# An ifftshift copied from memory to memory: 32 DMAs on two queues, or on one

## The chip, the cores and the metric

The kernel runs on one core of one Trainium2 chip. The metric is the time of one execution on the device, in microseconds (us). Two medians are compared, each over several runs.

## The reference

The input is an 8192 x 8192 array of 4-byte floats, 268.4 MB. The output has the same shape and holds the input with both halves of both axes exchanged:

```python
"x": np.random.randn(8192, 8192).astype(np.float32)

def reference(x):
    return np.fft.ifftshift(x)
```

For even sizes this means `out[r, c] = x[(r + 4096) % 8192, (c + 4096) % 8192]`. Nothing is calculated; every byte is read once and written once. One row is 32 KB and one half of a row 16 KB.

## The kernel before

No data enters the core's own memory. Every DMA reads from the device memory and writes to it. The 8192 output rows are cut into 32 blocks of 256 rows, and one DMA moves one block. Its two access patterns, each of the form [step, count] in elements, walk over 256 rows, then over the two halves of a row, then over the 4096 elements of a half. On the output side the halves go left, right. On the input side the walk starts at the right half and steps back by 4096 elements, so it goes right, left. The outermost count, 256, is shared out over the 16 DMA engines: 16 neighbouring rows each, which is 512 KB in 32 pieces of 16 KB.

The helper `whole_rows(queue, block, right_first)` issues one such DMA at L39; `right_first` is always `False` here, so its other branch is not used. The loop over `n` goes through the blocks in groups of four. The sync queue (SP) gets blocks n and n+1, the scalar queue (ACT) blocks n+2 and n+3:

```python
for n in range(0, blocks, 4):
    for a, b in ((0, 2), (1, 3)):
        whole_rows(nc.sync, n + a, False)
        whole_rows(nc.scalar, n + b, False)
```

Each queue thus issues 16 DMAs, and while SP's queue is at block n, ACT's is at block n+2, which is 2 x 8.39 MB further on in both arrays. Both queues feed the same 16 DMA engines. The DMAs don't depend on each other. The framework hands out eight completion semaphores in turn, four to each queue, and before a semaphore is used again the issuing queue waits for the DMA that used it last. So the fifth DMA of a queue waits for its first. At the end SP waits for all of them (L73).

Of the kernel before, what the change touches and what calls it, by code (L numbers as in the profile page):

```python
# [1 line left out]

# [4 lines left out]


ENGINES = 16


@with_exitstack
def kernel(
    ctx: ExitStack,
    tc: tile.TileContext,
    x: bass.AP,
    out: bass.AP,
):


    nc = tc.nc
    R, C = x.shape
    hr = R // 2
    hc = C // 2
    rows = ENGINES * 16
    blocks = R // rows

    def whole_rows(queue, block, right_first):
        row = block * rows
        src = (row + hr) % R  # L30
        to = [[C, rows], [hc, 2], [1, hc]]
        back = [[C, rows], [-hc, 2], [1, hc]]
        if right_first:
            dst, dims, of = hc, back, 0
            dims_of = to
        else:
            dst, dims, of = 0, to, hc
            dims_of = back
        queue.dma_start(  # L39
            out=bass.AP(out.tensor, out.offset + row * C + dst, dims),  # L40
            in_=bass.AP(x.tensor, x.offset + src * C + of, dims_of),
        )

    for n in range(0, blocks, 4):
        for a, b in ((0, 2), (1, 3)):
            whole_rows(nc.sync, n + a, False)
            whole_rows(nc.scalar, n + b, False)


# [1 line left out]
_INS = ['x']  # L51
_OUTS = [((8192, 8192), 'float32')]


# [23 lines left out]
```

## Time and profile before

| what | value |
|---|---|
| median of 3 runs | 865.58 us (865.28 to 866.03) |
| profiled execution, its own time | 868.85 us |
| its span, first to last instruction | 867.1 us |
| busy time of the compute engines | 0.2 us (POOL, four constants that nothing uses) |
| DMA packets | 16896, of which 512 are under 512 B |
| mean rate of the copy | 310 GB/s read, and as much written |

The profile counts every byte of the copy once in its GB/s; the page's line on memory traffic adds reading and writing. A packet is one piece of 16 KB as one of the 16 DMA engines handles it; the 512 small ones report the completions, 16 for each DMA. "q1" is SP's queue and "q10" is ACT's. In the views by windows, the last two columns are the mean busy share of the 16 DMA engines and the rate in GB/s in that stretch; a share slightly over 1.00 comes from packets that reach over the edge of a stretch.

### The profile page before, as it was taken

The numbers are of one execution on the slowest core, as the hardware profiler recorded it, in microseconds if no ns is written. First come the engines' busy times: TensorE is split into PE (matmuls) and PEld (weight loads), VectorE is DVE, ScalarE is ACT, GpSimd is POOL, SyncE is SP. The second block draws the span as 40 slices with busy tenths as digits, with TensorE's granted clock in tenths as the row PEclk, the third lists the DMA queues.
The fourth block names the chain that finished last, engine by engine and source line by source line (L and its number), as shares of the span: only waits on it lengthen the run. The fifth ranks groups of instructions, "written<-read, shape, count | busy, mean of one in ns | idle before, by whom it ended". The sixth has DMA issues, their size and how long they took to land. (4 is left out here: it accounts for less than half of the span.)

```text
span 867.1 us, 77 instructions
## 1 busy us (share of the span) xinstructions
POOL 0.2 (0%) x4
## 2 busy tenths in 40 slices
POOL 0000000000000000000000000000000000000000
DMA  9999999999999999999999999999999999999998
GB/s 280 313 314 305 313 318 312 309 314 309 311 310 315 311 308 305 320 311 313 310 312 316 311 308 313 306 313 310 311 311 314 311 311 317 311 308 309 305 311 273
DMA packets 16896, 268.44 MB, mean 310 GB/s; under 512 B 512, under 2 KB 512, under 8 KB 512
## 3 DMA queue, kind: packets, MB, share of 16 engines
q10 hardware_dynamic: 8448, 134.22, 49.8%
q1 hardware_dynamic: 8448, 134.22, 49.6%
HBM read 268.44 MB, written 268.44 MB: 619 GB/s over the span
## 5 line engine op out<-in xcount | busy, mean ns | idle before, releaser
L62 POOL MEMSET const-bfloat16-1.0<- 128x1 bf16 x1 | 0.1, 102 | 0.0
L62 POOL MEMSET const-uint8-127<- 128x1 uint8 x1 | 0.1, 102 | 0.0
L62 POOL MEMSET const-float32-0.0<- 128x1 f32 x1 | 0.1, 99 | 0.2 <-issue 0.2
L62 POOL MEMSET const-float32-1.0<- 128x1 f32 x1 | 0.1, 99 | 0.0
## 6 DMA issues: line engine op xcount, KB each, us to landing
out_dram<-in_x_dram SPq DMA_DIRECT2D x16, 8192.0 KB, 215.4
out_dram<-in_x_dram ACTq DMA_DIRECT2D x16, 8192.0 KB, 215.4
```

The lines of the kernel that those rows point to most:

```text
L62: nc = _bacc.Bacc("TRN2", target_bir_lowering=False, num_devices=1)
```

## The change

The helper and the grouping go. One loop over the 32 blocks in ascending order issues every DMA on the sync queue; ACT issues none. The access patterns of a block are those of before: the same rows, the same two halves in the same order, the same 16 rows to each engine. All eight completion semaphores now belong to SP's DMAs, so its ninth DMA waits for its first.

```diff
     rows = ENGINES * 16
-    blocks = R // rows
 
-    def whole_rows(queue, block, right_first):
-        row = block * rows
+    for row in range(0, R, rows):
         src = (row + hr) % R
...
-        queue.dma_start(
-            out=bass.AP(out.tensor, out.offset + row * C + dst, dims),
-            in_=bass.AP(x.tensor, x.offset + src * C + of, dims_of),
+        nc.sync.dma_start(
+            out=bass.AP(out.tensor, out.offset + row * C, [[C, rows], [hc, 2], [1, hc]]),
+            in_=bass.AP(x.tensor, x.offset + src * C + hc, [[C, rows], [-hc, 2], [1, hc]]),
         )
-
-    for n in range(0, blocks, 4):
-        for a, b in ((0, 2), (1, 3)):
-            whole_rows(nc.sync, n + a, False)
-            whole_rows(nc.scalar, n + b, False)
```

More of the change, by code (lines that the diff above doesn't have):

```diff
@@ L25 @@
     rows = ENGINES * 16
-    blocks = R // rows
-    def whole_rows(queue, block, right_first):
-        row = block * rows
+    for row in range(0, R, rows):
         src = (row + hr) % R
[L31 to L39, printed above, removed]
-            out=bass.AP(out.tensor, out.offset + row * C + dst, dims),
-            in_=bass.AP(x.tensor, x.offset + src * C + of, dims_of),
-        )
-    for n in range(0, blocks, 4):
-        for a, b in ((0, 2), (1, 3)):
-            whole_rows(nc.sync, n + a, False)
-            whole_rows(nc.scalar, n + b, False)
+        nc.sync.dma_start(
+            out=bass.AP(out.tensor, out.offset + row * C, [[C, rows], [hc, 2], [1, hc]]),
+            in_=bass.AP(x.tensor, x.offset + src * C + hc, [[C, rows], [-hc, 2], [1, hc]]),
+        )
 _INS = ['x']
```

## The prediction

> **What bounds the kernel now.** I began with the page's slices and queues, since nothing is computed:
>
> ```profile
> DMA  9999999999999999999999999999999999999998
> GB/s 280 313 314 305 313 318 312 309 314 309 311 310 315 311 308 305 320 311 313 310 312 316 311 308 313 306 313 310 311 311 314 311 311 317 311 308 309 305 311 273
> DMA packets 16896, 268.44 MB, mean 310 GB/s; under 512 B 512, under 2 KB 512, under 8 KB 512
> q10 hardware_dynamic: 8448, 134.22, 49.8%
> q1 hardware_dynamic: 8448, 134.22, 49.6%
> ```
>
> All 16 DMA engines are busy in every slice, and the two queues share them evenly. The end is set by how long one 16 KB packet occupies an engine: 99.4% of 16 x 867.1 us over 16,384 such packets is 0.84 us. So an idle queue is not what could be repaired here. What can change is the duration of a packet, up or down. The views of the chain and of the waits hold only the four unused constants and SP waiting for DMAs, so I went on to the rate in short stretches. First the two ends of the span, where one queue is alone:
>
> ```profile
> core 0: us, POOL busy (x), PEclk, DMA share, GB/s
> 0.00:2.20 2.20, 0.20 (x4) 1.00 0.20 37
> 2.20:5.40 3.20, 0.00 (x0) 1.00 0.89 307
> 5.40:14.20 8.80, 0.00 (x0) 1.00 1.02 333
> 14.20:27.20 13.00, 0.00 (x0) 1.00 1.00 291
> 860.70:862.70 2.00, 0.00 (x0) 1.00 1.04 295
> 862.70:864.70 2.00, 0.00 (x0) 1.00 0.94 295
> 864.70:867.10 2.40, 0.00 (x0) 1.00 0.11 34
> ```
>
> Up to 5.4 us nearly all packets are SP's, and after 862.7 us all large ones are ACT's. The two microseconds before 862.7 with both queues and the two after it with one have the same 295 GB/s. So one queue can keep the engines moving. Neither end shows that a second queue by itself adds rate.
>
> Then I asked where in a block the rate changes. Two rows give the places of the queues:
>
> ```profile
> start us, us, engine line op out<-in xcount [idle before <-releaser]
> 55.22 46.51 SPq L39 DMA_DIRECT2D out_dram<-in_x_dram  x1
> 60.39 46.02 ACTq L39 DMA_DIRECT2D out_dram<-in_x_dram  x1
> ```
>
> These are the fifth DMAs of the two queues, each held until the queue's first DMA had landed. ACT is 5.2 us behind SP, and one DMA of each queue takes about 54 us. So after each completion there are some 5 us in which SP's packets are at the beginning of a 512 KB piece per engine and ACT's still at the end of one. Half a block later there are again 5 us in which SP is in the second 256 KB and ACT in the first. The rest of the time both queues are in the same 256 KB half of their pieces. I laid windows over this: a short one of 4.8 us for the stretches with the queues in different halves, from 27.4 us on every 26.94 us, and a long one of 21.6 us for the time between. There are thirty of each up to 835 us; here are the first two and the last two:
>
> ```profile
> 27.40:32.20 4.80, 0.00 (x0) 1.00 1.03 338
> 32.40:54.00 21.60, 0.00 (x0) 1.00 0.99 300
> 54.30:59.10 4.80, 0.00 (x0) 1.00 0.98 321
> 59.30:80.90 21.60, 0.00 (x0) 1.00 1.00 305
> ...
> 781.80:786.60 4.80, 0.00 (x0) 1.00 1.04 338
> 786.80:808.40 21.60, 0.00 (x0) 1.00 1.00 303
> 808.70:813.50 4.80, 0.00 (x0) 1.00 0.96 304
> 813.70:835.30 21.60, 0.00 (x0) 1.00 1.02 309
> ```
>
> The thirty short ones have a mean of 328.0 GB/s (304 to 345), the thirty long ones 307.5 GB/s (300 to 315). The scatter of a mean of thirty is 1.7 and 0.6 GB/s, so the difference of 20 GB/s is no accident. The engines are as busy in both, so what changes is the packet's duration, and that depends on which addresses the two queues are at.
>
> The mix gives the whole run: (4.8 x 328.0 + 22.14 x 307.5) / 26.94 = 311.15 GB/s, and 268.435 MB at that rate take 862.7 us. The profiled execution took 868.85 us, so 6.15 us are start, end and what lies around the span. The median of the runs shown is 865.58 us, 0.99624 of the profiled time.
>
> **The change part by part.** *ACT's sixteen issues go to SP.* SP then issues 32, one after another:
>
> ```profile
> 0.73 0.66 SPq L39 DMA_DIRECT2D out_dram<-in_x_dram  x1
> 2.80 46.60 SPq L39 DMA_DIRECT2D out_dram<-in_x_dram  x1
> out_dram<-in_x_dram SPq DMA_DIRECT2D x16, 8192.0 KB, 215.4
> out_dram<-in_x_dram ACTq DMA_DIRECT2D x16, 8192.0 KB, 215.4
> ```
>
> A free issue takes 0.66 us. The fourth, at 2.8 us, took 46.6 us, until shortly before the first DMA landed: the queue was full, with three DMAs ahead of it. After the change one DMA takes about 27 us, because it has the engines to itself, and three of them are some 80 us of work ahead of the sequencer. The issues cost nothing under that cover. Without it they would cost at most 32 x 0.66 = 21 us. Start and end stay as they are: SP's first packet still starts at about 2.2 us, and the last packets again run from one queue alone, so I keep the 6.15 us.
>
> *The waits.* SP's ninth DMA now waits for its first, then the tenth for its second. With at most four in the full queue the first has long landed when the ninth is reached. Behind that wait stand only SP's later issues. Cost nothing, with the same cover.
>
> *The order of addresses.* This is the whole price. At any moment an engine works on a packet of one queue, before and after, so 16 packets are in work either way. Before, about eight belong to SP's place and eight to ACT's, and for 4.8 of 26.94 us these places are in different halves. After, all 16 are at one place, and stand in the same half except while the engines cross from one half to the next. That is the state of the long windows, 307.5 GB/s.
>
> How long a crossing lasts with one queue the trace does not show. From below: nothing, if all engines cross at once; then 268.435 MB / 307.5 GB/s = 873.0 us, with 6.15 us 879.1, by the median 875.8 us. From above: as large a share of the time as now, and the median stays at 865.6. I take one packet's duration, 0.84 us, for the engines are not in step to better than a packet. A half block then takes 13.64 us (16 x 256 KB at 307.5), and the rate is (0.84 x 328.0 + 12.8 x 307.5) / 13.64 = 308.8 GB/s. That makes 869.3 us, with 6.15 us 875.5, against 868.85: 0.76% more, a median of 872.2 us.
>
> The trace says that places 256 KB apart go faster together than places in the same 256 KB. The Trainium skill has a relative of this under "DMA: Bandwidth & Descriptors", section "Latency and other measured facts": copies whose rows lie 4 MiB apart run at about half the rate of those 512 KiB apart, and it infers that streams in step then meet in the same channels. No run here shows those pitches, and the halves of 256 KB seen above are finer than what it lists; it speaks against moving all engines to one place.
>
> **The rivals.** *Two queues collide, one does not: faster.* The loss in the long windows may come not from 16 packets in one half but from SP's and ACT's packets there, 16.8 MB apart, getting in each other's way. With one queue every engine reads two neighbouring halves of a row one after the other, and nothing else comes in between. The whole copy then runs at the rate of the short windows: 268.435 / 328.0 = 818.4, with 6.15 us 824.6, a median of 821.5 us. It decides from the point at which the single stream passes 311.15 GB/s. For it speaks the stretch 5.4 to 14.2 us, 333 GB/s while both queues were in the first half; something other than the half slows the later windows. Against it speaks that ACT alone at the end made 295 GB/s, and those engines were still 0.94 busy, which is 314 at full share and not 328.
>
> *The second queue is worth nothing and costs nothing: no change.* The engines are full with either; if the short windows are fast because engines pass a boundary and not because the queues are apart, one queue passes the boundaries as often for the same bytes. Then the median stays at 865.6 us. For it speak the equal 295 GB/s with two queues and with one. The Trainium skill, "DMA: Bandwidth & Descriptors", section "Issuing engines are not separate DMA queues", states this outright: DMAs of all issuing engines run on the same 16 DMA engines, and more issuing engines save only the time to initiate. Its first half agrees with the even shares of q1 and q10; the rate that depends on the queues' places does not fit its second half.
>
> *One place is worse than the same half: much slower.* In the long windows the queues are still 5 us apart, about three packets each, which spreads the 16 packets over two places. With one queue that is gone. An engine that runs ahead also finds no second queue to take a packet from. The nearest row is the slowest long window, 300 GB/s: 894.8 us, with 6.15 us 900.9, a median of 897.6 us. The stretch 14.2 to 27.2 us with 291 GB/s shows that lower rates exist, 925 us by the same steps; I leave that end out. Against it speaks the head of the span: SP alone, with all engines in step, gave 307 GB/s from 2.2 to 5.4 us with the start of the transfers in it.
>
> **How the numbers follow.** The forecast, slower by some 0.8%, gets 0.45, since it only carries on a state that the kernel is in for four fifths of its time. The faster rival, with all between its end and no change, gets 0.29; no change 0.09; much slower 0.17. About 0.2% is what a measurement of this kernel can tell from no change, 1.7 us. Faster is then 0.29, within 0.2% 0.09, slower 0.45 + 0.17 = 0.62. The forecast's own range is 868 to 877 us, from the two bounds of the crossing. For 8 in 10 the range goes halfway into the faster rival, to 843 us (half of 0.29 left out), and up to the much slower one's 897 us (some 0.05 beyond it).
>
> **What would show it.** If the forecast is right, the changed profile has one queue with 32 DMAs and 16,896 packets, a DMA row still at 9 throughout, slices between 305 and 312 GB/s, and no long and short windows: cutting a block's 27 us into its halves shows one rate but for a microsecond. SP's issues each end shortly before the DMA three ahead of them lands. It is wrong if the slices stand at 320 and more (two queues collided), at or below 300 (one place is worse than one half), or if the DMA row falls below 9, which would mean that a single queue leaves engines idle and the cover of the issues is gone.

## The result

The changed kernel is faster: a median of 856.89 us (856.55 to 858.62, 4 runs) against 865.43 us (864.65 to 866.03, 4 runs) of the kernel before. The ratio is 0.9906, with a 95% interval from 0.9889 to 0.9923. Forecast was 872.2 us, slower by 0.8%; the sign was wrong. The result lies between the faster rival (821.5 us) and no change. The profiled execution took 856.55 us with a span of 854.8 us. Of all runs below one, a run of the half passes at 835.76 us, was in a slower state, and its ratio leaves it out.

The page of the changed kernel, slices and queues:

```profile
DMA  9999999999999999999999999999999999999998
GB/s 291 313 316 314 314 318 317 311 315 317 311 318 311 316 316 314 317 313 320 315 320 316 311 317 320 318 316 317 317 313 316 313 314 320 317 315 315 319 311 282
DMA packets 16897, 268.44 MB, mean 314 GB/s; under 512 B 513, under 2 KB 513, under 8 KB 513
q1 hardware_dynamic: 16896, 268.44, 99.5%
out_dram<-in_x_dram SPq DMA_DIRECT2D x32, 8192.0 KB, 112.1
```

One queue moves everything, the engines are as full as before, and 32 of the 40 slices are higher than before, by some 4.5 GB/s on the mean of all. Most lie at 311 to 320 GB/s, above the 305 to 312 of the forecast and below the 320 that was to show the faster rival. So the gain is a shorter packet: 99.5% of 16 x 854.8 us over 16,384 packets is 0.83 us, before 0.84 us. The issues are hidden, as the forecast had it. Of SP's issues, here are the free first one and a stretch with the fourth and the one behind it:

```profile
0.73 0.66 SPq L29 DMA_DIRECT2D out_dram<-in_x_dram  x1
2.79 47.71 SPq L29 DMA_DIRECT2D out_dram<-in_x_dram  x2
```

The sequencer stands at a full queue here too, and the DMA row shows no gap.

Then the windows of the forecast, laid over the changed kernel. One DMA now takes 26.6 us, so a half of 256 KB per engine takes 13.3 us. Short windows of 1.8 us lie where the engines pass into the next half, long ones of 11.1 us between; there are 56 of each up to 774 us, of which the first two and the last two are:

```profile
core 0: us, POOL busy (x), PEclk, DMA share, GB/s
28.80:30.60 1.80, 0.00 (x0) 1.00 1.13 382
42.10:43.90 1.80, 0.00 (x0) 1.00 1.05 364
...
747.00:748.80 1.80, 0.00 (x0) 1.00 1.02 319
760.30:762.10 1.80, 0.00 (x0) 1.00 1.12 355
```

```profile
30.80:41.90 11.10, 0.00 (x0) 1.00 0.99 307
44.10:55.20 11.10, 0.00 (x0) 1.00 1.01 307
...
749.00:760.10 11.10, 0.00 (x0) 1.00 1.01 310
762.30:773.40 11.10, 0.00 (x0) 1.00 0.98 314
```

The short ones have a mean of 334.4 GB/s (273 to 428), the long ones 312.3 GB/s (298 to 322); the scatter of these means is 3.8 and 0.7. Windows of 1.6 us, laid at six places around the crossing, gave means of 331 to 337 GB/s, so the figure does not hang on one choice of place. The rate still rises at the crossings, and between them it is itself higher than before: 312.3 against 307.5 GB/s. Of these 4.8 GB/s about 1.2 belong to the execution that was profiled before, which at 868.85 us ran 0.4% above its median, while the one after ran at its own. That the packets' places decide the rate holds; that one queue in one half has the same rate as two queues in one half does not.

### The profile page after: what moved, and what is told of

The parts are those of the page before. It is cut to its first block, busy times and chain, and to the rows that moved or that the text cites. A ratio compares the mean times of both kernels' runs of the same rounds, so it can differ in the third digit from the quotient of the medians.

```text
span 854.8 us, 77 instructions
## 1 busy us (share of the span) xinstructions
POOL 0.2 (0%) x4
## 3 DMA queue, kind: packets, MB, share of 16 engines
q1 hardware_dynamic: 16896, 268.44, 99.5%
```

## The experiments

Each kernel was compared with the kernel before on its own chip, where that took from 861.7 to 869.4 us. So ratios are given, with their 95% intervals; medians compare safely only on one chip. The diffs show only the lines that matter. `copy(queue, row, dims)` stands for the DMA of the changed kernel with the given dimensions over rows.

**Halves: 8 rows to an engine.** Neighbouring engines then start 256 KB apart instead of 512 KB.

```diff
-    rows = ENGINES * 16
+    rows = ENGINES * 8
```

> One queue as after the change, but 128 rows a DMA and so 8 neighbouring rows (256 KB) to an engine, 64 DMAs. Theory 'halves' (packets spread over both 256 KB halves go at 328 to 335 GB/s): neighbouring engines now always stand in opposite halves, so the fast rate holds throughout, about 268.4/330 = 813 us and 6 us more, 815 to 822 us. Theory 'boundary' (the fast two packets come from beginning a new stretch, wherever the others are): the same share of fast packets as with 16 rows or a little more, 850 to 857 us.

Measured: 824.44 us, ratio 0.9485 [0.9462, 0.9508]. Its slices:

```profile
GB/s 297 326 325 326 324 325 332 330 324 328 331 327 331 326 324 329 326 335 328 324 324 329 331 326 319 330 330 330 333 324 332 330 328 330 325 331 328 328 332 298
```

The rate of the short windows before (328.0) has become the rate of nearly all slices. The time is a little over the 815 to 822 us of theory "halves" and far from the 850 to 857 us of theory "boundary". One number in the code brings 5.2% where the change brought 0.9%. With 4 rows:

```diff
+    rows = ENGINES * 4
```

> One queue, 4 neighbouring rows (128 KB) to an engine, 64 rows a DMA, 128 DMAs. Theory 'halves' with 256 KB as the size that matters: pairs of engines share a half, still eight engines in each, as with 8 rows an engine: 5% below before. If finer spreading helps as well: 6% below or more.

Measured: 823.77 us, 0.9557 [0.9539, 0.9574]. As with 8 rows, as far as two chips can be compared; finer spreading adds nothing that shows.

**Two queues, other distances.** First the changed kernel again, on the chip of this group.

> The changed kernel once more, beside the three two-queue kernels of this call, so that they are compared on one chip. Expected about 1% below the kernel before, as in the first comparison.

Measured: 848.89 us, 0.9861 [0.9844, 0.9878]. The change is worth 0.9% in the first comparison and 1.4% on this chip.

```diff
+    for n in range(0, R // rows, 2):
+        copy(nc.sync, n * rows, [[C, rows]])
+        copy(nc.scalar, (n + 1) * rows, [[C, rows]])
```

> Two queues, SP on the even blocks and ACT on the odd ones, 8.4 MB apart where before they were 16.8 MB apart. Theory 'two places' by distance: the time changes with the distance, away from that of before by 0.5% or more. Theory 'two queues': as before within 0.3%.

Measured: 861.33 us, 0.9997 [0.9986, 1.0008]. The next kernel puts SP on output rows 0 to 4095 and ACT on 4096 to 8191; its `shift`, the rows of an extra first DMA of ACT that moves all its later blocks on, is 0.

> Two queues, SP on the upper half of the output and ACT on the lower half, 134 MB apart, both starting at the beginning of their 512 KB pieces. Theory 'halves': the distance doesn't matter, the halves of 256 KB are the same most of the time as before, so as before within 0.3%.

Measured: 862.84 us, 1.0011 [0.9996, 1.0025]. From 8.4 MB to 134 MB the distance of the queues changes nothing.

```diff
-    shift = 0
+    shift = 10
     lower = [shift] * (shift > 0) + [rows] * ((hr - shift) // rows)
```

> As the unshifted kernel, but ACT's blocks begin 10 rows further on (8 rows are 256 KB, 2 rows make up for ACT's lag), so that the two queues stand in opposite 256 KB halves nearly all the time. Theory 'halves': the rate of the short windows of before throughout, 328 GB/s, about 820 to 825 us, 5% below the unshifted one. If the halves don't matter and only the passing of a boundary does: as the unshifted one within 1%.

Measured: 832.34 us, 0.9666 [0.9648, 0.9684]; 3.5% below the unshifted kernel, of 5% expected. Slices:

```profile
GB/s 300 315 326 320 328 330 324 329 325 331 328 324 328 327 323 320 322 328 326 325 329 321 326 324 330 331 326 329 324 331 328 321 325 320 321 328 327 321 317 275
```

Counted from the packets that each queue had finished, ACT was about 6.4 packets behind SP here, not 3.5. Of the 20 packets of shift 13.6 remain, so the queues were in different halves for 13.6 of every 16 packets: 0.85 x 328.0 + 0.15 x 307.5 = 324.9 GB/s, and the page's mean is 323. So theory "halves" fits two queues as well, and most of the shortfall is my estimate of the lag.

**Two places or two queues.** A two-queue kernel with less lag was to part these:

```diff
-    shift = 0
+    shift = 2
```

> Two queues, 134 MB apart, as the unshifted kernel that took as long as before, but ACT's blocks begin 2 rows further on, which makes up for its lag of 3.5 packets, so both queues pass the boundaries of 256 KB together. Theory 'second place': two places that are in step act like one, about 1.4% below before. Theory 'two queues': as before, or slightly slower since the fast stretches at the boundaries get shorter, 862 to 872 us.

Measured: 865.09 us, 1.0032 [1.0017, 1.0046]. The lag had grown again, to 6 packets, where the shift of 2 rows makes up for 4, so some 2 remained. That leaves the question open, though it speaks for "two queues". One queue that walks the addresses of two tells more. It issues DMAs of 16 rows, [[16 * C, ENGINES]], which give each engine one row, from two streams of blocks in turn:

```diff
+    for t in range(len(first) + lag):   # lag = 2
+        if t < len(first):
+            row_each(*first[t])         # blocks n, n + 1 of four
+        if t >= lag:
+            row_each(*second[t - lag])  # blocks n + 2, n + 3
```

> One queue only, but it walks the addresses as the two queues of before did: DMAs of 16 rows (one row to each engine, 16 rows apart), in turn from block n and, two rows behind, from block n+2. The exchange of the columns is in place. Theory 'second place in the same half' (what cost the kernel before 1% over the kernel after is that the packets in work come from two places): about 1.4% above its partner with one place. Theory 'two queues' (the change between two queues costs it): like its partner.

> The partner: the same DMAs of 16 rows in one queue, block after block, so that each engine walks its addresses exactly as after the change. If 512 small DMAs cost nothing: as after, about 1.4% below the kernel before. If their issue or completion shows: slower, and only the difference to the kernel with two places counts.

Measured: two places 852.04 us, 0.9890 [0.9870, 0.9910]; one place 851.70 us, 0.9888 [0.9860, 0.9917]. Their line of totals is the same in both traces:

```profile
DMA packets 24580, 268.50 MB, mean 316 GB/s; under 512 B 8192, under 2 KB 8192, under 8 KB 8192
```

A second place in the same half costs nothing that shows, as long as one queue visits both in turn, row by row. Both keep most of the gain of the change. The 512 small DMAs may cost some 0.3%: the changed kernel took 848.89 us on this chip. So what the kernel before paid is not its second place as such; what is left is something that comes with the second queue. It need not be the change of queue itself: a second queue can also alter the order in which an engine meets left and right halves, and one queue that changes places after each 16 KB piece, with the exchange of the columns, was not run. With longer lags, `lag = 8` and `lag = 4`:

> One queue, two places as in the kernel with 16-row DMAs and a lag of 2 rows (0.989 of before), but the second place 8 rows (256 KB) behind. Theory 'halves': opposite halves nearly always, 5% faster than with a lag of 2 rows, 0.94 of before. Theory 'halves plus a price of the second queue': also about 1% faster than the shifted kernel on two queues (0.967 of before), which stood mostly in opposite halves too. If one queue with two places gains nothing from halves: 0.989.

> The same with a lag of 4 rows (128 KB), about the distance of the two queues in the kernel with even and odd rows (0.948 of before). If places 128 KB apart are as good as 256 KB apart: 0.94 to 0.95. If only different halves count: they differ half of the time, 0.965.

Measured: 826.10 us, 0.9584 [0.9563, 0.9605], and 841.30 us, 0.9763 [0.9742, 0.9784]. A lag of 8 rows, 256 KB, brings 3.1 points over the 0.989 of a lag of 2, of the 5 expected. A lag of 4 rows brings 1.3 points, some two fifths of that, where different halves for half of the time would bring half; its 0.9763 lies above both sums, 0.94 to 0.95 and 0.965. The halves count in one queue too, and places 128 KB apart are not as good as places 256 KB apart. The lag of 8 rows is also 0.8% below the shifted kernel on two queues (0.9666), as a price of the second queue would have it. But that kernel stood in one half for 0.15 of the time, which by the sum above (324.9 against 328.0 GB/s) is worth 0.9%, so this pair does not decide.

**Sides of a row.** Two kernels leave the exchange of the columns out:

```diff
-            in_=bass.AP(x.tensor, x.offset + src * C + hc, [[C, rows], [-hc, 2], [1, hc]]),
+        dims = [[C, rows], [-hc, 2], [1, hc]]                   # one place; on both sides
+        dims = [[hc, 2 * rows], [2 * rows * C, 2], [1, hc]]     # two places; on both sides
```

> The partner of the kernel with two places: one queue, block after block, pieces of 16 KB, right half and then left half of each row; the exchange of the columns is left out here too. All theories: about 857 us, as after the change, if the exchange of columns itself has no price.

> One queue, but each engine's 16 KB pieces alternate between block n and block n+2, 16.8 MB apart, as the two queues of before made them do; the exchange of the columns is left out (halves go to the side that they come from). Theory 'two places': like before, 864 to 870 us, and slower than its partner with one place by some 1%. Theory 'two queues': like its partner with one place, about 857 us.

Measured: one place 830.74 us, 0.9550 [0.9513, 0.9586]; two places 832.43 us, 0.9582 [0.9547, 0.9616]. Two places cost nothing that shows here either. But all theories were wrong on the level: without the exchange the copy is some 3% faster than the changed kernel. The bytes, the queue and the 512 KB between engines are the same; only which half is read while which is written differs. With the exchange, a piece reads the right side and writes the left, and the next piece reads the left while, if the writes trail by about a piece, the left is still being written. Half passes take that away and keep the exchange:

```diff
+        for to in (0, hc):
+            nc.sync.dma_start(
+                out=bass.AP(out.tensor, out.offset + row * C + to, [[C, rows], [1, hc]]),
+                in_=bass.AP(x.tensor, x.offset + src * C + hc - to, [[C, rows], [1, hc]]),
+            )
```

> One queue, 16 rows to an engine, but first all left halves of a block's output rows and then all right ones, so that reads and writes never stand in the same 16 KB side of a row. Theory 'sides' (after the change, reading a side while the piece before is being written to the same side costs; without the exchange of columns the one-place kernel took 0.955 of before): about 0.955. If sides don't matter: as after the change, 0.986 to 0.991.

Measured: 825.20 us (median of all four runs), 0.9554 [0.9530, 0.9578], as theory "sides" has it and far from 0.986. Within a pass every read is on one side and every write on the other, while neighbouring engines still start 512 KB apart. Slices and totals:

```profile
GB/s 293 328 301 326 320 324 327 333 320 328 316 332 327 330 322 335 332 324 332 332 326 330 328 332 328 329 332 324 332 336 331 321 334 332 328 326 332 329 336 276
DMA packets 17408, 268.44 MB, mean 326 GB/s; under 512 B 1024, under 2 KB 1024, under 8 KB 1024
```

**When the second queue costs.** Three kernels on two queues: even and odd rows of one block, 8 rows to an engine, and half passes. The edit of the first:

```diff
+        copy(nc.sync, row, [[2 * C, rows // 2]])
+        copy(nc.scalar, row + 1, [[2 * C, rows // 2]])
```

> Two queues again, but in the same block of 256 rows: SP takes its even rows, ACT its odd ones, 8 rows to an engine, so both queues work within some 100 KB of each other at every engine. Theory 'two places' (what cost time before was that the queues' addresses lay 16.8 MB apart): like one queue, 855 to 859 us. Theory 'two queues' (changing between two queues costs time by itself, whatever the addresses): like before, 864 to 867 us.

> 8 rows to an engine, as the one-queue kernel that took 0.949 of before, but on two queues in the block order of before. Theory 'the second queue costs': about 1% more than with one queue, 0.958. If the price of the second queue exists only while all packets stand in one half: as with one queue, 0.949.

> The half passes of the last one-queue kernel (0.955 of before), on two queues in the block order of before, 16 rows to an engine. If the second queue's price after all is one of sides (the two queues bring reads and writes to the same side of a row): as with one queue, 0.955. If changing between queues costs by itself wherever all packets stand in one half: 1.1% more, 0.966.

Measured: even and odd rows 824.28 us, 0.9481 [0.9462, 0.9500], far below what either theory had; 8 rows 822.08 us, 0.9538 [0.9523, 0.9554]; half passes 822.36 us, 0.9535 [0.9512, 0.9558]. The slices of the last:

```profile
GB/s 304 327 321 331 330 325 329 330 330 332 325 330 331 326 329 329 326 328 333 319 332 330 332 331 330 327 326 332 328 332 330 330 333 330 329 323 335 328 334 270
```

None of them shows a price of its second queue. Half passes are the clean pair, on one chip: 0.9535 on two queues, 0.9554 on one, where the price would have given 0.966. The 8 rows lie between both sums, 0.958 with the price and 0.949 without, and their partner on one queue (0.9485) ran on another chip. The fast kernels took 822 to 826 us on all three chips while the kernel before took 861.7 to 869.4 us, so part of such a difference in ratio comes from the kernel before; in microseconds it is 822.08 on two queues against 824.44 on one. So the second queue's price of about 1% was seen only where the packets meet in one half with mixed sides, and that changing between two queues costs by itself, whatever the addresses, is not borne out.

**Both gains together.** Half passes with 8 rows to an engine, one queue:

```diff
-    rows = ENGINES * 16
+    rows = ENGINES * 8
```

> One queue, half passes and 8 rows to an engine, both gains together. If sides and halves are separate causes whose gains add: 0.92 to 0.93 of before. If both lead to the same limit: 0.95 to 0.956, like either alone.

Measured: 823.83 us, 0.9580 [0.9553, 0.9607]. They don't add. Halves, sides, and even and odd rows all end at 325 to 327 GB/s by the page, 822 to 826 us. Any of these beats both kernels; the simplest is 8 rows to an engine on one queue.

## Why the prediction was wrong

*What bounds the kernel* was right: the duration of a packet, engines full before and after, decided by addresses. The fast and the slow windows were real, and the experiment that kept the packets in different halves throughout got the rate of the short ones.

*The issues and the waits cost nothing*: right; the DMA row of the profile after shows no gap, and even 512 issues cost some 0.3%, if anything, beside the changed kernel on the same chip (851.70 against 848.89 us). *Start and end* were 856.55 us less 851.4 us of copying, 5.2 us instead of 6.15.

*The order of addresses* is where the sum failed, in its step "After, all 16 are at one place, and stand in the same half except while the engines cross from one half to the next. That is the state of the long windows, 307.5 GB/s." I let a rate measured with two queues stand for one queue. The long windows after have 312.3 GB/s. The second term, the length of a crossing, was too small as well: about 1.8 us at 334.4 GB/s where I took 0.84 us at 328.0. With the crossing alone mended, (1.8 x 334.4 + 11.5 x 307.5) / 13.3 = 311.1 GB/s and the copy takes 862.8 us instead of 869.3; with the rate of the long windows too, 315.3 GB/s and 851.4 us. So 6.5 us of the error come from the crossing and 11.4 us from the rate between crossings, and the second turned the sign. With the profiled execution before put at its median (308.7 for 307.5 GB/s) the second is still 8.5 us.

A hint lay in the rows of the end of the span, which the prediction called equal: 295 GB/s at a DMA share of 1.04 with two queues and of 0.94 with one are 284 and 314 GB/s at full share. The 314 was used only against the faster rival. Two microseconds prove little, but the changed kernel's single queue then made 312.3 GB/s between crossings and 315.3 in all. The forecast's own range, 868 to 877 us, does not follow from its two bounds either, which were 865.6 and 875.8 us. That 856.89 us lies in the wide range, 843 to 897 us, is owed to the share given to the faster rival and not to the forecast's mechanism.

*The faster rival* had the right direction, and its reason was right in part. It had SP's and ACT's packets, 16.8 MB apart, get in each other's way; the distance does nothing (0.9997 and 1.0011), nor do two places in one queue. Its price assumed that the collision was the whole loss in the long windows. In fact the second queue made about a fifth of it, (312.3 - 307.5) / (328.0 - 307.5) = 0.23, or 0.18 with the execution before at its median. The rest goes with the packets of all 16 engines in one half and reads and writes on mixed sides, for it vanishes when either is taken away, and it remains after the change. *No change* is excluded by the interval, 0.9889 to 0.9923. *Much slower* is refuted: one place is no worse than two.

The Trainium skill, "DMA: Bandwidth & Descriptors", section "Issuing engines are not separate DMA queues", has all issuing engines on the same 16 DMA engines, so that a second one brings no bandwidth. The half passes agree (0.9535 on two queues, 0.9554 on one). The change itself goes further: there the second queue cost 0.9 to 1.4%. In the same page, "Latency and other measured facts", the row pitch at large powers of two is said to lower the rate. The halves resemble that, with a size that the skill doesn't list: engines 512 KB apart took 0.986 to 0.991 of before, engines 256 KB apart 0.949. But the distance of the engines alone does not decide, for half passes kept the 512 KB and took 0.955; that both have one cause is not shown.

What stays open is how the second queue costs 1% where sides are mixed, and why even and odd rows on two queues escape it although both queues are in one half for about three fifths of the time, counted from their packets. Their distance does not explain it, since one queue with places 128 KB apart took 0.9763; that the two queues keep to rows of different parity was not tested by itself. That reads and writes on the same side meet somewhere in the memory is an inference from which orders are fast; no view shows the inside of the memory. How far the writes trail the reads was not measured.

## What to carry to other kernels

When a copy keeps all DMA engines full, its rate can still depend on which addresses are in work together: look at the rate in short windows laid over the period of the access pattern, and then try the pattern's pitch and order before the queues. A rate seen under one condition carries over to a changed kernel only if everything else that makes up the condition stays; here the number of queues was part of it. Engines spread over 256 KB, or reads and writes kept on opposite sides of a row, were each worth 4 to 5% against the 0.9 to 1.4% of the choice of the queue, and together no more than one alone.

## What the runs showed that was not expected

A copy that exchanges the halves of each row piece by piece ran 3% slower than one without the exchange, at equal bytes, and half passes won that back (0.9554). The fast orders that keep the exchange all end at 325 to 327 GB/s by their pages, with the engines still full. DMAs of 512 KB, 512 of them on one queue, cost little against 32 of 8 MB (0.989 against 0.986 on the same chip).
